# Block 1's attention of a two-block transformer: 64-wide heads handled in pairs on the two array halves

## The chip, the core and the metric

The kernel runs on one core of one Trainium2 chip. The metric is the device time of one execution in microseconds; before the change the median of three runs is 2548.09 us.

## What is computed

Two transformer blocks follow one another on one sequence of 256 tokens of width 2048, in float32. The change touches the first block's attention alone: 16 heads of width 64, whose query chunk of 64 tokens sees up to 9 chunks of 64 keys, with a bias by relative distance. Cut to that part:

```python
h = rms_norm(x, norm_mix_w)
q_a, k_a, v_a, q_g, k_g, v_g, r_g, gate_lr = split_cols(h @ w_in, IN_SPLITS)
# chunked_band_attention, for each chunk c of 64 queries:
s = einsum('bqhd,bkhd->bhqk', qc, kb) * 64 ** -0.5 + bias     # invalid keys: float32's minimum
y_a = einsum('bhqk,bkhd->bqhd', softmax(s), vb)
...
x = x + concatenate([y_a, y_g], axis=-1) @ w_out
# feed forward with a causal convolution, gated embedding; then the second block:
# 8 heads of rotary attention, 8 heads of retention, feed forward, gated embedding
```

With 256 tokens all keys fit: queries 0 to 127 need keys 0 to 127, queries 128 to 255 need keys 0 to 255.

## The kernel before

Every weight is read once from HBM, in 881 tiles of 128 x 1024 numbers at most (`weight_plan`). A tile passes through three stages: SyncE loads it into `raw` (`load`, L148, four buffers), ScalarE copies it to `wh`, rounded to the product format fp32r (`split_hi`, L156, five buffers), and VectorE stores what is left in `wl` (`split_lo`, L167, four buffers). TensorE then multiplies both parts with the activations, which are split in the same way, and sums in PSUM tiles `acc` (`mm`, L222). In `prod_a` (wide tiles of 2 k-tiles and 512 columns) a tile takes 12 products of 512 columns, in `prod_b` 16 of 512 and 256.

The order of all work is that of the Python program. `slot` stands at the start of each weight tile `i`: it emits the rounding of tile `i + 4`, the remainder of tile `i + 3`, the load of tile `i + 7`, and then one `tick`, before the products of tile `i`. A tick takes one step of up to two evictions (`ev`) and one step of the first generator in `side`. Attention is such a generator: its instructions stand in every engine's queue between the work of two weight tiles, and each `yield` passes on to the next tile. Every engine runs its queue in order.

Block 1's mixer (`mix1`) first makes the values, keys and queries of a gated linear attention and runs that as side work (`gla`, whose step `second` holds products with 64-row operands and whose step `third` has products with 64-column weights), then makes `qT` and `kT` (the transposed queries and keys; two heads of 64 share one 128-partition block) and starts `att1`, while the weight products for `va` (the values) and for the gate `rg` run. In one step `s` of `att1` three heads are at work:

- `late` first runs what was put off: the normalisation of the probabilities of head `s - 1` (`softmax`'s `rest`, VectorE, L640 and L642), and the low part of a finished `y1a` block (L667).
- `turn(s - 2)` transposes the probabilities `aP` on TensorE (three transposes, L650) into the one `tr` bank of PSUM, and ScalarE copies them to `aT` (L652).
- `scores(s)` makes the scores of head `s` in a bank `sc` (two banks): 128 and 256 columns on one 64-row half of the array. VectorE adds the bias `aB` and takes the maximum (L628), ScalarE takes the exponential with its sum (L635).
- `values(s - 4)` multiplies with `va`: 256 and 128 columns, with 64-column weights, into one half of the partitions of `pv`; after an odd head ScalarE copies the block to `aV` and rounds it to `y1a` (L663, L664).

`fetch` brings the bias of a pair of heads (L586) and masks a corner on GpSimd (L587). The buffers: `aP`, `aT` and `aB` two, `ast` (the small statistics) three. `softmax` and `turn` are used by block 2's attention too, and block 2 uses the tag `aP` for `qkn` and `sT`.

Of the kernel before, what the change touches and what calls it, by code (L numbers as in the profile page):

```python
# [12 lines left out]
P = 128  # L13
T = 256
# [4 lines left out]
FMIN = float(np.finfo(np.float32).min)  # L19
# [3 lines left out]


def weight_plan():
    """The weight tiles in the order of use: (k-tiles, column ranges).

    Wide tiles have 2 k-tiles of 512 columns (moving operand), narrow ones
    4 k-tiles of 256 columns (stationary operand).
    """  # L30
    tiles = []
    full = tuple(range(KT))

    def gemm(n, kts, chunks):
        for ch in chunks:
            for i in range(0, len(kts), n):
                tiles.append((kts[i : i + n], ch))

    def even(name, lo, hi, step):
        return [[(name, c, c + step)] for c in range(lo, hi, step)]  # L40

    def wide(name, lo, hi):
        gemm(2, full, even(name, lo, hi, 512))

    def narrow(name, lo, hi, kts=full):
        gemm(4, kts, even(name, lo, hi, 256))

    def ffn(gate, up, off, down):
        for a, b in HALVES:
            gemm(4, full, [[(gate, c * P, c * P + P), (up, off + c * P, off + c * P + P)] for c in range(a, b)])  # L50
            narrow(down, 0, D, tuple(range(a, b)))

    def ple(gate, proj):
        for c in range(0, D, 512):
            narrow(gate, c, c + 512)
            gemm(2, (0, 1), even(proj, c, c + 512, 512))

    gemm(2, full, [[("w_in", 4096, 4608)], [("w_in", 4608, 4864)], [("w_in", 4864, 5120), ("w_in", 6144, 6160)]])
    narrow("w_in", 3072, 4096)
    narrow("w_in", 0, 2048)  # L60
    wide("w_in", 2048, 3072)
    wide("w_in", 5120, 6144)
    narrow("w_out", 0, D, MIX_ORDER)
    ffn("w_ffn_up", "w_ffn_up", FF, "w_ffn_down")
    ple("w_ple_gate", "w_ple_proj")
    wide("w_in_2", 0, 3072)
    narrow("w_in_2", 3072, 5120)
    wide("w_in_2", 5120, 7168)
    narrow("w_o_2", 0, D)
    ffn("w_gate_2", "w_up_2", 0, "w_down_2")  # L70
    ple("w_ple_gate_2", "w_ple_proj_2")
    return tiles
# [25 lines left out]
class Net:  # L98
# [14 lines left out]
        self.nacc = 0  # L113
        self.forced = []

# [1 line left out]
    def t(self, tag, shape, dt=F32, bufs=1, name=None):  # L117
        return self.sp.tile(shape, dt, tag=tag, name=name or tag, bufs=bufs)

# [12 lines left out]
    def pv(self):  # L132
        return self.psum("pv", 1)

# [1 line left out]
    def cut(self, i, part):  # L136
        f = self.offs[i][1]
        return slice(0, f) if part is None else slice(part * f // 2, (part + 1) * f // 2)
# [37 lines left out]
        assert len(self.plan[i][0]) == nk  # L176
        return self.H.pop(i), self.L.pop(i), self.offs[i][1] // nk

# [1 line left out]
    def step(self, q, g):  # L180
        try:
            next(g)
# [27 lines left out]
        while key not in self.done:  # L210
            yield

# [1 line left out]
    def begin_chunk(self):  # L214
        c = self.nacc
        self.nacc += 1
# [48 lines left out]
                    self.mm(o, x[:, ls], H[:, sl], False, g + j == nk - 1)  # L265

    def join(self, acc, dst):
        """dst = the sum of both halves of a narrow chunk's accumulators."""
        m = self.v2(self.t("tq", [P, 512], bufs=2))
        self.nc.scalar.activation(m, acc[:, :, T:], AF.Copy)  # L270
        yield
        self.nc.vector.tensor_add(dst, m, acc[:, :, :T])
# [4 lines left out]

        self.ev.append(self.freeing(c, evict(acc)))

# [1 line left out]
    def v2(self, ap):  # L281
        return ap.rearrange("p (b t) -> p b t", b=2)

# [79 lines left out]

        return rc, rb, run()

# [1 line left out]
    def consts(self):  # L367
        nc, ins = self.nc, self.ins
        self.vec = self.t("vec", [P, NV])
# [75 lines left out]
        while self.ev or self.side:  # L445
            self.tick()

# [1 line left out]
    def mix1(self, acts):  # L449
        nc = self.nc  # L450
        rc, rb = self.rc, self.rb
# [125 lines left out]

    def att1(self, qT, kT, va, Y0):
        nc = self.nc
        bias, Pm, PT, st = {}, {}, {}, {}  # L580
        late = []

        def fetch(g):
            if g < 8:
                b = self.t("aB", [P, 2, T], bufs=2)
                nc.sync.dma_start(b, self.ins["bias"][:, 2 * g : 2 * g + 2, :])  # L586
                nc.gpsimd.memset(b[0:64, :, 192:256], FMIN)  # L587
                bias[g] = b

        def scores(h):  # L590
            if h % 2 == 0:
                fetch(h // 2 + 1)
            b = bias[h // 2][:, h % 2, :]
            hp, blk = slice((h % 2) * 64, (h % 2) * 64 + 64), h // 2
            s = self.sc()
            self.mm(s[:, 0:128], qT[hp, blk, 0:128], kT[hp, blk, 0:128], True, True)
            self.mm(s[:, 128:384], qT[hp, blk, 128:256], kT[hp, blk, :], True, True)
            late.append(self.softmax(h, s, [b[:, 128:256], b], FMIN, Pm))

        fetch(0)  # L600
        yield from self.wait(("kT", 3))
        yield
        yield
        for s in range(21):
            if s >= 4:
                yield from self.wait(("va", min(s - 4, 15) // 8))
            while late:
                late.pop(0)()
            if 2 <= s < 18:
                self.turn(s - 2, Pm, PT)  # L610
            if s < 16:
                scores(s)
            if 4 <= s < 20:
                h = s - 4
                if h % 2 == 0:
                    st["pv"] = self.pv()
                self.values(h, PT, va, st["pv"][(h % 2) * 64 : (h % 2) * 64 + 64], slice(h * 64, h * 64 + 64))
                if h % 2 == 1:
                    late.append(self.hilo_plain(Y0, h // 2, st["pv"][:, :T], "y"))
            yield  # L620

    def softmax(self, h, s, masks, floor, Pm, scale=(None, None)):
        nc = self.nc
        p = self.t("aP", [P, 384], bufs=2)
        st = self.t("ast", [P, 8], bufs=3)
        segs = ((0, 128), (128, 384))
        for i, (a, b) in enumerate(segs):
            nc.vector.tensor_tensor_reduce(p[:, a:b], s[:, a:b], masks[i], 1.0, floor, ALU.add, ALU.max, st[:, i : i + 1])  # L628
        if scale[0] is None:
            nc.vector.tensor_scalar(st[:, 2:4], st[:, 0:2], -1.0, None, ALU.mult)  # L630
        else:
            for i in range(2):
                nc.vector.tensor_scalar(st[:, 2 + i : 3 + i], st[:, i : i + 1], scale[i], -1.0, ALU.mult, ALU.mult)
        for i, (a, b) in enumerate(segs):
            nc.scalar.activation(p[:, a:b], p[:, a:b], AF.Exp, bias=st[:, 2 + i : 3 + i],  # L635
                                 scale=1.0 if scale[i] is None else scale[i], accum_out=st[:, 4 + i : 5 + i])
        Pm[h] = p

        def rest():
            nc.vector.reciprocal(st[:, 6:8], st[:, 4:6])  # L640
            for i, (a, b) in enumerate(segs):
                nc.vector.tensor_scalar(p[:, a:b], p[:, a:b], st[:, 6 + i : 7 + i], None, ALU.mult)  # L642
        return rest

    def turn(self, h, Pm, PT):
        nc = self.nc
        p = Pm.pop(h)
        t = self.tr()
        for i in range(3):
            nc.tensor.transpose(t[:, i * P : i * P + P], p[:, i * P : i * P + P], self.ident)  # L650
        o = self.t("aT", [P, 384], bufs=2)
        nc.scalar.activation(o, t[:, :384], AF.Copy)  # L652
        PT[h] = o

# [132 lines left out]
        self.done.add(("go", 3))  # L787
        yield

# [1 line left out]
    def ffn(self, blk):  # L791
        nc = self.nc
        hk = self.hkey
# [79 lines left out]
            yield from self.put_g(G, gk, cl, w[:, 1, :])  # L873
        return ev

# [1 line left out]
    def embed(self, blk):  # L877
        nc = self.nc
        s8 = self.t("S8a", [P, 2, 1024], name="pr")
# [92 lines left out]
            yield  # L972
        self.done.add(("ple", blk, c))

# [1 line left out]
    def rope_tables(self):  # L976
        nc, ins = self.nc, self.ins
        tabs = self.tabs = self.t("g4", [P, 4, 2, P], name="tabs")
        ra = self.t("tq", [P, 512], bufs=2, name="ropeA")
        ra = ra.rearrange("p (s t d) -> p s t d", s=2, t=2)  # L980
        nc.sync.dma_start(ra, ins["ropeA"])
        qk = self.t("aP", [P, 384], bufs=2, name="qkn")[:, :T].rearrange("p (a d) -> p a d", a=2)
        nc.sync.dma_start(qk, ins["qkn"])
        for _ in range(8):
            yield
        for i in range(2):
            nc.vector.tensor_mul(tabs[:, 2 * i], ra[:, 0], self.bc2(qk[:, i, :]))
            for h in range(2):
                a, b = slice(h * 64, h * 64 + 64), slice(64 - h * 64, 128 - h * 64)
                nc.vector.tensor_mul(tabs[:, 2 * i + 1, :, a], ra[:, 1, :, a],  # L990
                                     qk[:, i, b].unsqueeze(1).broadcast_to([P, 2, 64]))
            yield
# [231 lines left out]
    def ret2(self, R4, rv, st):  # L1224
        nc = self.nc
        o = self.t("S8a", [P, 2, 1024], name="ro")
# [15 lines left out]
        def decayed(h):  # L1242
            fetch(h + 1)
            dk = dks.pop(h)
            q, k = R4[:, 0, h], R4[:, 1, h]
            s = self.sc()
            self.mm(s[:, 0:256], k[:, 0:128], q[:, :], True, True)
            self.mm(s[:, 256:384], k[:, 128:256], q[:, 128:256], True, True)
            d = self.t("aP", [P, 384], bufs=2, name="sT")
            nc.vector.tensor_mul(d, s[:, :384], dk)  # L1250
            sT[h] = d

# [119 lines left out]
```

## Time and profile before

| | us |
|---|---|
| three runs | 2547.77, 2548.09, 2548.92 |
| span of the profiled execution (the page gives no other time of it) | 2547.2 |
| TensorE busy | 2534.5 |
| VectorE busy | 1668.3 |
| ScalarE busy | 1282.9 |
| DMA, mean | 184 GB/s |
| block 1's attention as side work | 218.7 to 317 of the span |

The span runs from the first to the last instruction of one profiled execution. Times inside it count from its start. In a timeline a row is one instruction, or several of one kind in a row (x3), with its start and length; matmuls overlap, so the distance from start to start tells what one costs, not its length. Each float32 product appears as two matmuls (two passes), a product in fp32r as one.

### The profile page before, as it was taken

The page shows a single profiled execution, that of the slowest core. Times are in us where ns is not written, and L with a number is a line of the kernel's source. Part 1 is how long each engine was busy: PE and PEld are TensorE (multiplying, and loading weights), DVE is VectorE, ACT ScalarE, POOL GpSimd, SP SyncE. Part 2 cuts the span into 40 slices and gives each one's busy share as a digit, 9 for nine tenths or more (in the row PEclk, how much of TensorE's full clock was granted, in tenths as well). Part 3 has the DMA queues.
Part 4 walks back from the last instruction along what each step waited for, and adds up shares of the span by engine and source line. Part 5 has one row for each costly group of instructions (what it writes and reads, how often), then busy time and mean ns, then how long its engine had stood idle before and what let it go on. Part 6 is the DMA issues. An engine that isn't in the chain of part 4 may idle for free.

```text
span 2547.2 us, 36496 instructions
## 1 busy us (share of the span) xinstructions
PE 2534.5 (100%) x14162; PEld 2184.4 (86%) x14162; DVE 1668.3 (65%) x2374; ACT 1282.9 (50%) x1713; POOL 8.3 (0%) x60
## 2 busy tenths in 40 slices
PE   8999999999999999999999999999999999999999
PEld 7887788888888888888878888888888888888888
DVE  6655567777755777767886775666666555666665
ACT  6534544655543565545544544444444334444443
POOL 0000000000000000000000000000000000000000
PEclk9999999999999999999999999999999999999999
DMA  7545355555555555555555455555555555555554
GB/s 242 183 142 178 131 177 188 187 186 190 190 189 188 186 190 190 192 193 187 189 174 188 161 177 189 174 187 189 188 188 189 190 190 189 187 188 193 190 193 147
DMA packets 133550, 469.30 MB, mean 184 GB/s; under 512 B 14960, under 2 KB 17392, under 8 KB 133376
## 3 DMA queue, kind: packets, MB, share of 16 engines
q1 hardware_dynamic: 133232, 466.95, 54.1%
q8 instruction: 111, 1.82, 0.3%
q14 instruction: 63, 0.52, 0.1%
q10 hardware_dynamic: 144, 0.01, 0.0%
HBM read 464.80 MB, written 2.10 MB: 183 GB/s over the span
## 4 chain that ended last, share of the span: by engine, by line
PE 99%; DMA 0%; DVE 0%; ACT 0%; issue 0%; SPq 0%; ACTq 0%
PE acc L222 95%; PE sc L222 2%; PE pv L222 1%; PE tr L650 0%; DMA raw<-weights 0%; PE sc L1099 0%; ACT wh L156 0%; PE sc L1182 0%; PE sc L528 0%; DVE ty L948 0%; SPq L390 0%; DVE wl L167 0%; DVE X L949 0%; PE tr L737 0%; SPq L148 0%
## 5 line engine op out<-in xcount | busy, mean ns | idle before, releaser
L167 DVE TENSOR_TENSOR wl<-raw,wh 128x1024 fp32r<-128x1024 f32 (+1 forms) x881 | 1068.8, 1214 | 830.6 <-PE acc L222 538.6
L156 ACT ACTIVATE wh<-raw 128x1024 fp32r<-128x1024 f32 (+1 forms) x881 | 924.7, 1050 | 905.7 <-PE acc L222 729.8
L222 PE MATMUL acc<-f,wh 128*128 128x512 f32 x2816 | 984.3, 393 | 0.0
L222 PE MATMUL acc<-f,wl 128*128 128x256 f32 x2816 | 786.2, 279 | 0.0
L222 PEld LDWEIGHTS acc<-f,wh 128*128 128x128 f32 x2816 | 528.0, 187 | 123.9
L222 PEld LDWEIGHTS acc<-f,wl 128*128 128x128 f32 x2816 | 528.3, 188 | 0.0
L222 PE MATMUL acc<-g,wh 128*128 128x512 f32 x1408 | 491.0, 393 | 0.0
L222 PE MATMUL acc<-g,wl 128*128 128x256 f32 x1408 | 393.2, 279 | 0.0
L222 PEld LDWEIGHTS acc<-g,wh 128*128 128x128 f32 x1408 | 264.1, 188 | 61.1
L222 PEld LDWEIGHTS acc<-g,wl 128*128 128x128 f32 x1408 | 264.3, 188 | 0.0
L222 PE MATMUL acc<-hp,wh 128*128 128x512 f32 x512 | 179.9, 394 | 0.0
L222 PE MATMUL acc<-hp,wl 128*128 128x256 f32 x512 | 143.0, 279 | 0.0
L222 PEld LDWEIGHTS acc<-hp,wh 128*128 128x128 f32 x512 | 96.0, 188 | 22.2
L222 PE MATMUL acc<-wh,m2b 128*128 128x512 f32 x320 | 104.5, 398 | 0.0
L222 PE MATMUL acc<-wh,m2a 128*128 128x512 f32 x320 | 104.4, 399 | 0.0
L222 PEld LDWEIGHTS acc<-hp,wl 128*128 128x128 f32 x512 | 96.1, 188 | 0.0
L849 ACT ACTIVATE ty<-tU,vec 128x256 f32<-128x256 f32 x88 | 48.1, 595 | 75.1 <-DVE tU L845 75.1
L270 ACT ACTIVATE tq<-acc 128x512 f32<-128x512 f32 x124 | 71.9, 580 | 4.9 <-PE acc L222 4.9
L222 PE MATMUL acc<-wh,h0a 128*128 128x512 f32 (+2 forms) x224 | 68.1, 380 | 5.7 <-ACT wh L156 5.7
L222 PEld LDWEIGHTS acc<-wh,m2a 128*128 128x128 f32 x320 | 60.3, 188 | 14.2
L222 PEld LDWEIGHTS acc<-wh,m2b 128*128 128x128 f32 x320 | 60.1, 188 | 14.1
L222 PE MATMUL acc<-h0a,wh 128*128 128x512 f32 x192 | 68.6, 397 | 0.0
(272 smaller groups left out, 2780.6 us busy)
## 6 DMA issues: line engine op xcount, KB each, us to landing
raw<-weights SPq DMA_DIRECT2D x863, 512.0 KB, 3.4
raw<-weights SPq DMA_DIRECT2D x10, 256.0 KB, 2.8
raw<-weights SPq DMA_DIRECT2D x8, 272.0 KB, 2.8
aB<-bias SPq DMA_DIRECT2D x8, 256.0 KB, 3.5
X<-xT SPq DMA_DIRECT2D x7, 256.0 KB, 6.6
dk<-decay SPq DMA_DIRECT2D x8, 192.0 KB, 3.7
out<-X SPq DMA_DIRECT2D x6, 256.0 KB, 2.8
pr<-pT SPq DMA_DIRECT2D x2, 256.0 KB, 4.2
```

Of the source, the lines that this page charges most:

```text
L156: self.nc.scalar.activation(self.H[i][:, a], self.raw[i][:, a], AF.Copy)
L167: self.nc.vector.tensor_sub(self.L[i][:, a], r[:, a], self.H[i][:, a].bitcast(F32))
L222: self.nc.tensor.matmul(out, lhsT, rhs, start=start, stop=stop, skip_group_check=True, **kw)
L270: self.nc.scalar.activation(m, acc[:, :, T:], AF.Copy)
L849: nc.scalar.activation(y[:, b, :], u[:, b, 0:T], AF.Identity, scale=self.col("cw0", j), bias=self.col("b_ffn_conv", j))
```

## The change

`att1` now works on pairs. `scores(g)` takes both `sc` banks and issues the 256 columns of head 2g, those of head 2g + 1, and then the 128 columns of each; the two heads lie on the two row halves of the array. `values(g)` does so with the two column halves. A round `g` takes two ticks: the first holds the put-off normalisations, one `turn` and a pair of scores, the second a pair of values and one `turn`. `aP` and `aT` get four buffers, `ast` six. The rest of the diff removes comments and sets a smaller scratch for descriptors of software-made DMAs.

```diff
-        bias, Pm, PT, st = {}, {}, {}, {}
+        bias, Pm, PT = {}, {}, {}
...
-        def scores(h):
-            if h % 2 == 0:
-                fetch(h // 2 + 1)
-            b = bias[h // 2][:, h % 2, :]
-            hp, blk = slice((h % 2) * 64, (h % 2) * 64 + 64), h // 2
-            s = self.sc()
-            self.mm(s[:, 0:128], qT[hp, blk, 0:128], kT[hp, blk, 0:128], True, True)
-            self.mm(s[:, 128:384], qT[hp, blk, 128:256], kT[hp, blk, :], True, True)
-            late.append(self.softmax(h, s, [b[:, 128:256], b], FMIN, Pm))
+        def scores(g):
+            fetch(g + 1)
+            pair, sss = (2 * g, 2 * g + 1), []
+            for h in pair:
+                sss.append((self.sc(), slice((h % 2) * 64, (h % 2) * 64 + 64)))
+            for qs, ks, o in ((slice(128, 256), slice(0, 256), slice(128, 384)), (slice(0, 128), slice(0, 128), slice(0, 128))):
+                for s, hp in sss:
+                    self.mm(s[:, o], qT[hp, g, qs], kT[hp, g, ks], True, True)
+            for h, (s, _) in zip(pair, sss):
+                b = bias[g][:, h % 2, :]
+                late.append(self.softmax(h, s, [b[:, 128:256], b], FMIN, Pm))
+
+        def values(g):
+            o = self.pv()
+            ps = [PT.pop(h) for h in (2 * g, 2 * g + 1)]
+            for t, (lo, ks) in enumerate(((0, slice(0, 256)), (P, slice(256, 384)))):
+                for j in range(2):
+                    h = 2 * g + j
+                    self.mm(o[j * 64 : j * 64 + 64, lo:T], va[:, t, h * 64 : h * 64 + 64], ps[j][:, ks], t == 0, t == 1)
+            late.append(self.hilo_plain(Y0, g, o[:, :T], "y"))
...
-        for s in range(21):
-            if s >= 4:
-                yield from self.wait(("va", min(s - 4, 15) // 8))
+        for g in range(10):
             while late:
                 late.pop(0)()
-            if 2 <= s < 18:
-                self.turn(s - 2, Pm, PT)
-            if s < 16:
-                scores(s)
-            if 4 <= s < 20:
-                h = s - 4
-                if h % 2 == 0:
-                    st["pv"] = self.pv()
-                self.values(h, PT, va, st["pv"][(h % 2) * 64 : (h % 2) * 64 + 64], slice(h * 64, h * 64 + 64))
-                if h % 2 == 1:
-                    late.append(self.hilo_plain(Y0, h // 2, st["pv"][:, :T], "y"))
-            yield
+            if g >= 2:
+                self.turn(2 * g - 3, Pm, PT)
+            if g < 8:
+                scores(g)
+            yield
+            if g >= 2:
+                yield from self.wait(("va", (g - 2) // 4))
+                values(g - 2)
+            if 1 <= g < 9:
+                self.turn(2 * g - 2, Pm, PT)
+            yield
+        while late:
+            late.pop(0)()
...
-        p = self.t("aP", [P, 384], bufs=2)
-        st = self.t("ast", [P, 8], bufs=3)
+        p = self.t("aP", [P, 384], bufs=4)
+        st = self.t("ast", [P, 8], bufs=6)
...
-        o = self.t("aT", [P, 384], bufs=2)
+        o = self.t("aT", [P, 384], bufs=4)
...
-    nc = _bacc.Bacc("TRN2", target_bir_lowering=False, num_devices=1)
+    nc = _bacc.Bacc("TRN2", target_bir_lowering=False, num_devices=1, dynamic_dma_scratch_size=2048)
```

The order of instructions is written by the program, so the rows below show what moves. TensorE's queue before, one tick in the middle of the attention, between the products of two weight tiles (`tr` transposes, `sc` scores, `pv` values, `acc` weight products; a float32 product is one row here):

```order
L222 MATMUL acc<-wh,h0b 128x512
L650 MATMUL tr<-ident,aP 128x128 x3
L222 MATMUL sc<-qk_138 128x128
L222 MATMUL sc<-qk_138 128x256
L222 MATMUL pv<-aT,va 64x256
L222 MATMUL pv<-aT,va 64x128
L222 MATMUL acc<-wh,h0b 128x512
```

The same queue after the change, first a tick with a pair of values:

```order
L222 MATMUL acc<-wh,h0b 128x512
L222 MATMUL pv<-aT,va 64x256 x2
L222 MATMUL pv<-aT,va 64x128 x2
L660 MATMUL tr<-ident,aP 128x128 x3
L222 MATMUL acc<-wh,h0b 128x512
```

and the next, with a pair of scores:

```order
L222 MATMUL acc<-wh,h0b 128x512
L660 MATMUL tr<-ident,aP 128x128 x3
L222 MATMUL sc<-qk_138 128x256 x2
L222 MATMUL sc<-qk_138 128x128 x2
L222 MATMUL acc<-wh,h0b 128x512
```

Two ticks that each held the transposes, scores and values of one head have become one with the values of two heads and one with the scores of two; each keeps one head's transposes.

ScalarE's queue before, one tick of the same part in which a block of `y1a` is finished (`wh` the rounding of a weight tile, `aP` exponentials, `aT` the copy of transposes, `aV` and `y1a` the finished block):

```order
L156 ACTIVATE wh<-raw 128x1024
L652 ACTIVATE aT<-tr 128x384
L635 ACTIVATE aP,ast<-aP,ast 128x128
L635 ACTIVATE aP,ast<-aP,ast 128x256
L663 ACTIVATE aV<-pv 128x256
L664 ACTIVATE y1a<-aV 128x256
L156 ACTIVATE wh<-raw 128x1024
```

and after, from the score tick on through the value tick:

```order
L156 ACTIVATE wh<-raw 128x1024
L662 ACTIVATE aT<-tr 128x384
L645 ACTIVATE aP,ast<-aP,ast 128x128
L645 ACTIVATE aP,ast<-aP,ast 128x256
L645 ACTIVATE aP,ast<-aP,ast 128x128
L645 ACTIVATE aP,ast<-aP,ast 128x256
L156 ACTIVATE wh<-raw 128x1024
L473 ACTIVATE va<-acc,rc 128x512
L673 ACTIVATE aV<-pv 128x256
L674 ACTIVATE y1a<-aV 128x256
L662 ACTIVATE aT<-tr 128x384
```

The exponentials of two heads stand together behind the score tick's copy, and the next `wh` and the value tick's copies stand behind both; the row of `va` is an eviction that falls into this pair of ticks and not into most.

## Rows read from the trace of the kernel before

**Rows 1.** The page, busy time by engine and the chain that ended last, by engine.
```profile
PE 2534.5 (100%) x14162; PEld 2184.4 (86%) x14162; DVE 1668.3 (65%) x2374; ACT 1282.9 (50%) x1713; POOL 8.3 (0%) x60
...
PE 99%; DMA 0%; DVE 0%; ACT 0%; issue 0%; SPq 0%; ACTq 0%
```

**Rows 2.** Timeline of TensorE, one middle tick; columns start us, length us, instruction.
```profile
262.81 0.39 PE L222 MATMUL acc<-wh,h0b 128*128 128x512 f32 x1
263.04 0.49 PE L650 MATMUL tr<-ident,aP 128*128 128x128 f32 x3
263.46 0.92 PE L222 MATMUL sc<-qk 64*128 64x128 f32 x4
264.31 0.86 PE L222 MATMUL pv<-aT,va 128*64 128x256 f32 x4
265.10 0.50 PE L222 MATMUL acc<-wh,h0b 128*128 128x512 f32 x1
265.44 0.40 PE L222 MATMUL acc<-wl,h0b 128*128 128x512 f32 x1
```

**Rows 3.** Timeline of TensorE, an early tick with scores alone.
```profile
222.25 0.39 PE L222 MATMUL acc<-wh,h0a 128*128 128x512 f32 x1
222.58 0.92 PE L222 MATMUL sc<-qk 64*128 64x128 f32 x4
```

**Rows 4.** Timeline of TensorE, products with 64-row operands in the gated linear attention.
```profile
127.73 0.48 PE L222 MATMUL pv<-vg,gke 64*128 64x256 f32 x1
127.73 0.48 PE L222 MATMUL tr<-vg,gke 64*128 64x256 f32 x1
128.05 0.38 PE L222 MATMUL pv<-vg,gke 64*128 64x256 f32 x1
128.06 0.38 PE L222 MATMUL tr<-vg,gke 64*128 64x256 f32 x1
128.26 0.59 PE L222 MATMUL pv<-vg,gke 64*128 64x256 f32 x2
128.79 0.50 PE L222 MATMUL acc<-h0a,wh 128*128 128x512 f32 x1
```

**Rows 5.** Timeline of TensorE, products with 64-column weights in the gated linear attention.
```profile
136.13 1.08 PE L222 MATMUL sc<-gS,gla 128*64 128x256 f32 x6
137.13 0.50 PE L222 MATMUL acc<-h0b,wh 128*128 128x512 f32 x1
```

**Rows 6.** Timeline of VectorE, one slot, and the start of the next.
```profile
263.06 1.23 DVE L167 TENSOR_TENSOR wl<-raw,wh 128x1024 fp32r<-128x1024 f32 x1 [2.33 <-PE acc L222]
264.20 0.16 DVE L640 RECIPROCAL ast<-ast 128x2 f32<-128x2 f32 x1
...
264.86 0.42 DVE L667 TENSOR_TENSOR y1a<-aV,y1a 128x256 fp32r<-128x256 f32 x1
265.20 0.28 DVE L628 CUSTOM_DVE_ANT_0 aP<-sc,aB 128x128 f32<-128x128 f32 x1
...
265.87 0.17 DVE L630 TENSOR_SCALAR ast<-ast 128x2 f32<-128x2 f32 x1
268.04 1.23 DVE L167 TENSOR_TENSOR wl<-raw,wh 128x1024 fp32r<-128x1024 f32 x1 [2.00 <-PE acc L222]
```

**Rows 7.** Timeline of ScalarE, an eviction of va, and later one slot.
```profile
238.68 0.66 ACT L473 ACTIVATE va<-acc,rc 128x512 f32<-128x512 f32 x1
...
258.26 1.06 ACT L156 ACTIVATE wh<-raw 128x1024 fp32r<-128x1024 f32 x1 [1.15 <-PE acc L222]
260.23 0.49 ACT L652 ACTIVATE aT<-tr 128x384 f32<-128x384 f32 x1 [0.91 <-PE pv L222]
260.76 0.40 ACT L635 ACTIVATE aP<-aP,ast 128x128 f32<-128x128 f32 x1
...
261.65 0.36 ACT L663 ACTIVATE aV<-pv 128x256 f32<-128x256 f32 x1
262.05 0.42 ACT L664 ACTIVATE y1a<-aV 128x256 fp32r<-128x256 f32 x1
```

**Rows 8.** DMA issues of the page, the bias; the last number is us to landing.
```profile
aB<-bias SPq DMA_DIRECT2D x8, 256.0 KB, 3.5
```

More of the change, by code (lines that the diff above doesn't have):

```diff
@@ L981, in rope_tables @@
         nc.sync.dma_start(ra, ins["ropeA"])
-        qk = self.t("aP", [P, 384], bufs=2, name="qkn")[:, :T].rearrange("p (a d) -> p a d", a=2)
+        qk = self.t("aP", [P, 384], bufs=4, name="qkn")[:, :T].rearrange("p (a d) -> p a d", a=2)
         nc.sync.dma_start(qk, ins["qkn"])
@@ L1248, in decayed @@
             self.mm(s[:, 256:384], k[:, 128:256], q[:, 128:256], True, True)
-            d = self.t("aP", [P, 384], bufs=2, name="sT")
+            d = self.t("aP", [P, 384], bufs=4, name="sT")
             nc.vector.tensor_mul(d, s[:, :384], dk)
```

## The prediction

> **What bounds the kernel now.** The page comes first: TensorE is busy for 2534.5 of 2547.2 us and holds 99% of the chain that ended last [rows 1]. So a microsecond counts only if it leaves TensorE's own row of work, or adds a wait to it. The change sits in one stretch, block 1's attention (218.7 to 317 us), where the attention runs as side work between the weight products: before each weight tile's 12 products (`acc`, one every 0.23 us, 2.8 us for a tile) TensorE does one tick of attention. I call a tile with its tick a slot. The timeline of TensorE alone shows what a tick costs, read from start to start. Middle slot [rows 2]: from the last product at 262.81 to the transposes 0.23, so no loss; three transposes to the scores 0.42; the scores of one head 0.85; the values of one head 0.79; then the second product comes 0.34 after the first, 0.11 later than usual, because its weights were not loaded ahead. Entering scores straight from a product costs 0.33 instead of 0.23, that is 0.10 [rows 3]. The short attention products thus pay about 0.1 for every change between full-array and half-array work, on the way in and on the way out, beside the columns they stream.
>
> The question that decides is whether two half-array products run at once. The kernel before already has such a place, the gated linear attention [rows 4]. There three products with 64-row operands are issued one whole product after another, each in two passes: `pv` on the lower rows, `tr` on the upper rows, `pv` on the lower rows again. The trace has the first passes of `pv` and `tr` both at 127.73 and the second ones at 128.05 and 128.06, and the third product follows at 128.26. Six passes of 256 columns are over at 128.79, after 1.06 us; in a row they would need about six times 0.215 (the step from 128.05 to 128.26 is 0.21), 1.29, and the changes of mode on top. The same stretch has three products with 64-column weights that write alternate halves of PSUM's partitions: six passes in 1.00 us from 136.13 to 137.13 [rows 5], four passes' worth. So both kinds of pair (rows for scores, columns for values) run in step on this chip.
>
> **The change, part by part.**
> *Scores and values.* `scores(g)` issues 256 columns of head 2g, then of 2g+1, then 128 and 128, in two PSUM banks and the two row halves; `values(g)` does the like in the two column halves. By rows 4 a pair should take the path of one head: 0.85 for scores, 0.79 for values. That halves 16 x 0.85 + 16 x 0.79.
> *Ticks.* Before, with the prices above, the 20 ticks that hold work are: 2 of scores alone (0.10+0.85+0.11 = 1.06), 2 of transposes and scores (0.42+0.85+0.11 = 1.38), 12 of all three (0.42+0.85+0.79+0.11 = 2.17), 2 of transposes and values (0.42+0.79+0.11 = 1.32), 2 of values alone (0.10+0.79+0.11 = 1.00). Sum 2.12+2.76+26.04+2.64+2.00 = 35.56 us. After: 2 ticks of a score pair alone (2.12), 6 of transposes and a score pair (8.28), 3 of transposes alone (0.42 less the 0.10 that a mode change takes, 0.96), 7 of a value pair and transposes, 1 of a value pair alone (1.00). The 7 have the order values, transposes, which no row shows; between 0.10+0.79+0.32 = 1.21 (nothing lost behind) and 1.32 I take 1.32, the price of the same two pieces the other way round, as one entry and one exit remain: 9.24. Sum 21.60. **The ticks give 13.96 us**; some 10.4 of it (16 pairs, each with 2 x 0.215 + 2 x 0.108 = 0.65 of streaming that now runs beside the other head's; 128 columns take half of 256) is overlap, the other 3.6 fewer changes of mode.
> *Transposes.* All 16 stay, each with its copy to `aT`; they move by at most a slot.
> *VectorE.* It does the same work, but both heads' softmax now stands in every second slot, behind that slot's `wl`. From a slot's start [rows 6]: `wl` 1.14, two normalisations of 0.66, the low part of y 0.34, two mask-and-maximum steps of 0.84 (0.67 to the start of the last instruction, which takes 0.17). The first head's scores are ready for the exponential at 3.65, the second's at 4.50. The next slot's `wl` starts about 0.3 late; it is prepared three tiles ahead, so that costs nothing. Per pair of slots VectorE needs 5.6 of 8.3 us (two slots of 2.8, plus 1.38 and 1.32).
> *ScalarE.* A head's exponentials take 0.89 [rows 7], so they end near 5.5; then come `wh` (1.06), `aV` (0.40), `y1a` (0.42) and the copy of the other head's transposes (0.49): the end is near 7.9. What waits for it is TensorE: the single `tr` bank must be empty before the next slot's transposes at 8.3. Cover 0.4 us. In one pair the copy of `va` (0.66) stands in between and overruns this by about 0.3; with a little for the signal I charge **0.4 us**, and between nothing and 2 us for all such waits in the range.
> *Four buffers.* Before, `aT` stood behind the values of the same tick because it had two buffers: 0.9 us of idle ScalarE [rows 7]. With four this wait goes. TensorE did not wait for that copy, so it gives nothing by itself; it is what lets ScalarE fit the shorter slot. In block 2 the softmax, `sT` and `aT` share these tags; TensorE is the chain there too [rows 1], so nothing.
> *Bias.* The 256 KB of a pair's bias are still fetched one pair ahead and land in 3.5 us [rows 8], now with two slots of 4.1 us to do it; on SyncE's queue the fetches stand one or two weight loads from where they stood. Nothing. The smaller scratch for software-made DMA descriptors: no such queue in the profile, nothing.
>
> Sum: 13.96 - 0.4 = 13.6 us. The profiled span of 2547.2 would become 2533.6; the median of the three runs, 2548.09, lies 0.9 above that span, so the forecast is **2534.5 us**. Everything behind shifts forward as it is, since TensorE stays the chain.
>
> **The rivals.**
> *Passes start in program order.* Then only the second pass of one head overlaps the first of the next. A pair then streams first | second and other first | other second and first of the 128 | ... , three steps of 0.215 and two of 0.108 in place of two and two: 0.215 more a pair, 16 x 0.215 = 3.4 us, 2537.9. Against it: rows 4 have `tr`'s first pass 0.32 before `pv`'s second, though `pv`'s was issued first. The Trainium skill states this order (TensorE: Matmul & The Clock Gate, Part 3: Packing small matmuls): matmuls start and end strictly as issued. Here the trace differs from it by those 0.32 us, and the sum goes by the trace. Chance 4%.
> *ScalarE holds the single `tr` bank.* If its chain ends 1 us later than worked out, TensorE waits 0.6 at the transposes; the wait itself lengthens that slot and gives the next pair its cover back, so it comes in every second of 7 pairs: some 2.4 us, 2536.9. For it: only 0.4 us of cover. Against: the terms are measured ones, and ScalarE idles earlier in the pair. 10%.
> *No overlap at all*, so that the pairing is only another order: the path of a score pair becomes 0.85 + 6 x 0.108 = 1.50, of a value pair 1.44; the 16 pairs take back 10.4 us, and 3.2 remain, 2544.9. Rows 4 and 5 speak against. 3%.
> *Slower.* The bias of a pair comes late: VectorE's queue is in order, so the first mask step would hold the next `wl` behind it, and when three tiles of lead are used up TensorE waits. A fetch issued about 1.3 into its slot has until 8.3 + 2.8 = 11.1, near 10 us against 3.5 measured. To undo the gain, each of the 7 later pairs must lose 2 us, so each fetch would have to take some 20 us (10, the lead of about 8, and 2); at 2.7 us lost per pair it is 7 x 2.7 - 13.6 = 5.3 us slower, 2553.4. 2%.
>
> **How the numbers follow.** The forecast holds with 81%, and its own range is 2533.0 to 2536.5 (below: no waits, 0.4, the cheaper order in the 7 ticks, 0.8, and the 0.3 by which the lowest run lies under the median; above: waits of 2 us more). Widened to take in the two milder rivals it is **2533.0 to 2539.0**. What a measurement here can tell from no change is about 0.2%, 5.1 us: the forecast, program order and the `tr` bank all gain more, so faster 0.95; no overlap at all is the same, 0.03; slower 0.02.
>
> **What would show it.** In the changed kernel's timeline, a score pair: passes of both heads starting within 0.02 us of each other, and the next product 0.85 after the first; a value pair 0.79; slots of 4.2 and 4.1 us where 4.98 stood (from `wl` to `wl`, [rows 6]); ScalarE's last copy of a pair ending before the next transposes; TensorE's busy time down by about 13 us. Score passes that start one after another, or a row of waits of TensorE for `aT`, would prove the sum wrong, and a gap before `sc` with VectorE's mask step waiting for the bias the last rival.

## The result, and the profile after

The changed kernel took 2535.19 us in the median of four runs (2530.89, 2532.18, 2538.2, 2539.07), the kernel before beside it 2548.26 (2547.77 to 2548.92, four runs). The ratio is 0.9948, interval 0.9934 to 0.9962: faster by 13.1 us. The four runs of the changed kernel lie on two levels some 7 us apart, though the granted clock is 0.999 or 1.0 in all of them; the experiments come back to this. The profiled execution, 2530.89 us with a span of 2529.1, is one of the lower level.

The page of the changed kernel, busy time by engine, the chain that ended last, and the bias:

```profile
PE 2517.6 (100%) x14162; PEld 2177.6 (86%) x14162; DVE 1667.8 (66%) x2374; ACT 1279.3 (51%) x1713; POOL 8.4 (0%) x60
...
PE 99%; DMA 0%; DVE 0%; ACT 0%; issue 0%; SPq 0%; ACTq 0%
...
aB<-bias SPq DMA_DIRECT2D x8, 256.0 KB, 3.6
```

TensorE stays the chain, and the time left its own work: 2534.5 us busy [rows 1] became 2517.6, 16.9 less, for a span 18.1 shorter. The bias lands as before [rows 8].

The timeline of TensorE, a score tick and the value tick after it, and the start of the next pair:

```profile
251.57 0.39 PE L222 MATMUL acc<-wh,h0b 128*128 128x512 f32 x1
251.80 0.49 PE L660 MATMUL tr<-ident,aP 128*128 128x128 f32 x3
252.22 0.92 PE L222 MATMUL sc<-qk 64*128 64x256 f32 x8
253.07 0.50 PE L222 MATMUL acc<-wh,h0b 128*128 128x512 f32 x1
253.41 0.39 PE L222 MATMUL acc<-wl,h0b 128*128 128x512 f32 x1
...
255.72 0.39 PE L222 MATMUL acc<-wh,h0b 128*128 128x512 f32 x1
256.04 0.87 PE L222 MATMUL pv<-aT,va 128*64 128x256 f32 x8
256.84 0.55 PE L660 MATMUL tr<-ident,aP 128*128 128x128 f32 x3
257.14 0.48 PE L222 MATMUL acc<-wh,h0b 128*128 128x512 f32 x1
257.45 0.39 PE L222 MATMUL acc<-wl,h0b 128*128 128x512 f32 x1
...
259.98 0.49 PE L660 MATMUL tr<-ident,aP 128*128 128x128 f32 x3
```

Eight passes of scores, two heads, take 0.85 us from 252.22 to 253.07: as long as the four passes of one head before [rows 2]. Eight passes of values take 0.80. A pair of slots is 8.18 us long (251.80 to 259.98); two slots before took twice 4.98.

VectorE in the same pair: the remainders `wl`, and between them the last instruction of the second head's mask step.

```profile
251.83 1.23 DVE L167 TENSOR_TENSOR wl<-raw,wh 128x1024 fp32r<-128x1024 f32 x1 [2.62 <-PE acc L222]
...
256.05 0.17 DVE L640 TENSOR_SCALAR ast<-ast 128x2 f32<-128x2 f32 x1
256.15 1.22 DVE L167 TENSOR_TENSOR wl<-raw,wh 128x1024 fp32r<-128x1024 f32 x1
260.01 1.22 DVE L167 TENSOR_TENSOR wl<-raw,wh 128x1024 fp32r<-128x1024 f32 x1 [2.63 <-PE acc L222]
```

Both heads' mask steps fill the first slot to the end, so the second `wl` starts late, at once behind them; the third waits for TensorE again. The slots measured from `wl` to `wl` are 4.32 and 3.86, and nobody waits for the late one.

ScalarE at the end of the same pair:

```profile
257.27 1.04 ACT L156 ACTIVATE wh<-raw 128x1024 fp32r<-128x1024 f32 x1
258.22 0.36 ACT L673 ACTIVATE aV<-pv 128x256 f32<-128x256 f32 x1
258.62 0.42 ACT L674 ACTIVATE y1a<-aV 128x256 fp32r<-128x256 f32 x1
258.94 0.47 ACT L662 ACTIVATE aT<-tr 128x384 f32<-128x384 f32 x1
```

The copy out of the `tr` bank ends at 259.41, 0.57 ahead of the transposes at 259.98. The waits of TensorE's weight loads in the attention (us in total, times, longest) show where that cover did not do:

```profile
PEld tr L660 <- ACT aT L662: 0.7, 2, 0.3
```

**Where the time went, stage by stage.** The attention is only part of it. These rows of TensorE's timeline give the first product of the first feed forward, of block 2's mixer (`m2a`), of its output projection (`y2a`), of the second feed forward and of the second embedding (`hp`). The kernel before:

```profile
426.56 0.40 PE L222 MATMUL acc<-f,wh 128*128 128x512 f32 x1
...
1267.34 0.40 PE L222 MATMUL acc<-wh,m2a 128*128 128x512 f32 x1
...
1612.22 0.39 PE L222 MATMUL acc<-y2a,wh 128*128 128x512 f32 x1
...
1702.83 0.39 PE L222 MATMUL acc<-f,wh 128*128 128x512 f32 x1
...
2440.36 0.40 PE L222 MATMUL acc<-hp,wh 128*128 128x512 f32 x1
```

The changed kernel:

```profile
409.14 0.39 PE L222 MATMUL acc<-f,wh 128*128 128x512 f32 x1
...
1250.19 0.40 PE L222 MATMUL acc<-wh,m2a 128*128 128x512 f32 x1
...
1592.73 0.39 PE L222 MATMUL acc<-y2a,wh 128*128 128x512 f32 x1
...
1682.56 0.39 PE L222 MATMUL acc<-f,wh 128*128 128x512 f32 x1
...
2422.31 0.39 PE L222 MATMUL acc<-hp,wh 128*128 128x512 f32 x1
```

Up to the first feed forward it is 17.4 us ahead, more than the 13.6 forecast; 2.1 of that lie ahead of the first score product (216.57 against 218.72), before any instruction that the change moves. Block 2's mixer, where no instruction moved, then takes 342.54 us (1592.73 - 1250.19) where it took 344.88, and the second feed forward 739.75 where it took 737.53. Stages that the order does not touch changed their pace in both directions, so the prediction's sum cannot be checked against the total alone.

### The profile page after: what moved, and what is told of

Its sections match the earlier page's. It is cut to its first block, busy times and chain, and to the rows that moved or that the text cites. A ratio compares the mean times of both kernels' runs of the same rounds, so it can differ in the third digit from the quotient of the medians.

```text
span 2529.1 us, 36486 instructions
## 1 busy us (share of the span) xinstructions
PE 2517.6 (100%) x14162; PEld 2177.6 (86%) x14162; DVE 1667.8 (66%) x2374; ACT 1279.3 (51%) x1713; POOL 8.4 (0%) x60
## 4 chain that ended last, share of the span: by engine, by line
PE 99%; DMA 0%; DVE 0%; ACT 0%; issue 0%; SPq 0%; ACTq 0%
PE acc L222 95%; PE sc L222 2%; PE pv L222 1%; PE tr L660 0%; DMA raw<-weights 0%; PE sc L1109 0%; ACT wh L156 0%; PE sc L1192 0%; PE sc L528 0%; DVE ty L958 0%; SPq L390 0%; DVE wl L167 0%; DVE X L959 0%; PE tr L747 0%; SPq L148 0%
```

## Experiments

The kernels were measured in three groups (e1 to e4; e5, e6, e7 and e9; e10 to e13), each beside the kernel before and on one chip; medians are given, with the ratio and its interval. The theory was that the order of the pairs gains what the prediction's sum says, by overlap of the two halves; the rivals, that the issue order within a pair, the additional buffers or the place of the buffers in memory made or hid some of it.

### The change again, twice

No edit.

> The changed kernel once more, unaltered. Its four runs lay at 2530.9, 2532.2, 2538.2 and 2539.1 us, while the kernel before keeps within 1.2 us. Theory A (the gain is the ticks of the attention alone, 13.6 us, and the spread is chance): runs spread evenly around 2535. Theory B (beside the ticks, the pace of the weight products changed, and it has two levels): runs fall into two groups near 2531 and 2538.5, with little between.

> The change unaltered, in another call. If the two levels seen so far (2531 in two of the first runs, 2538 in the others) belong to the chip or its day: one level throughout, 2538 or 2531. If they are drawn anew for each loading of the program: both levels among the runs.

Measured: 2538.27 (2537.81 to 2539.72, five runs; before 2547.75; 0.9965, 0.9951 to 0.9978), and on another chip 2538.99 (2537.98 to 2541.0, five runs; before 2548.1; 0.9965, 0.9953 to 0.9978). Both times only the upper of the two levels. Of the second, the three last stage starts:

```profile
1593.87 0.39 PE L222 MATMUL acc<-y2a,wh 128*128 128x512 f32 x1
...
1685.29 0.40 PE L222 MATMUL acc<-f,wh 128*128 128x512 f32 x1
...
2430.53 0.39 PE L222 MATMUL acc<-hp,wh 128*128 128x512 f32 x1
```

Output projection and second feed forward together took 836.66 us here and 829.58 in the changed kernel's first profile; the 7.1 us between the levels lie in these two stages. With ten more runs on the upper level, the first four runs' median of 2535.19 reads as a mixture: two runs near 2531.5 and two near 2538.6.

### The larger buffers without the new order

The scratch alone (e2), and the old order with the change's scratch and buffers (e3):

```diff
-    nc = _bacc.Bacc("TRN2", target_bir_lowering=False, num_devices=1)
+    nc = _bacc.Bacc("TRN2", target_bir_lowering=False, num_devices=1, dynamic_dma_scratch_size=2048)
```

and for e3 also

```diff
-        p = self.t("aP", [P, 384], bufs=2)
-        st = self.t("ast", [P, 8], bufs=3)
+        p = self.t("aP", [P, 384], bufs=4)
+        st = self.t("ast", [P, 8], bufs=6)
...
-        o = self.t("aT", [P, 384], bufs=2)
+        o = self.t("aT", [P, 384], bufs=4)
```

> The kernel before with the smaller descriptor scratch alone. Theory A: 2548.3 within 0.5 us, one level. Theory B (where the tiles lie in SBUF sets the pace of the products, and this edit moves them): another level than 2548, by up to 4 us either way, or two levels.

> The kernel before, attention head by head in the old order, with the smaller scratch and the larger buffer counts (aP 4, aT 4, ast 6), so with the memory map of the changed kernel. Theory A: 2548 within 0.5 us, since TensorE waited for none of these buffers. Theory B: about 4 us less (2544) in the good level, as the products over h0a then take 0.227 us in place of 0.235, and about 2551 in the other.

Measured: e2 2548.16 (eleven runs; 1.0003, 0.9994 to 1.0011), nothing. e3 2552.48 (2551.48 to 2555.09, eleven runs; 1.002, 1.0011 to 1.0028): **the buffers alone cost 4.7 us**. One theory had expected no change, the other 4 us less or 3 more. Against e3, the change measured beside it (e1) is 14.2 us faster. So the new order gains about 14, and something that came with the buffers takes a third of it back.

### Head by head instead of alternately

The pair's products in the order of the heads, as a program that knows nothing of the halves would issue them:

```diff
-            for qs, ks, o in ((slice(128, 256), slice(0, 256), slice(128, 384)), (slice(0, 128), slice(0, 128), slice(0, 128))):
-                for s, hp in sss:
+            for s, hp in sss:
+                for qs, ks, o in ((slice(128, 256), slice(0, 256), slice(128, 384)), (slice(0, 128), slice(0, 128), slice(0, 128))):
...
-            for t, (lo, ks) in enumerate(((0, slice(0, 256)), (P, slice(256, 384)))):
-                for j in range(2):
+            for j in range(2):
+                for t, (lo, ks) in enumerate(((0, slice(0, 256)), (P, slice(256, 384)))):
```

> The changed kernel, but within a pair both products of the first head are issued before both of the second, in scores and in values. If TensorE starts the second head only when its passes come up in the order of issue, a score pair goes from 0.85 to about 1.4 us and a value pair from 0.80 to about 1.35, 16 x 0.55 = 8.8 us more: about 2544. If the two halves have queues of their own that look far enough ahead, the time is that of the changed kernel, 2531 to 2539, with the passes of both heads in step.

Measured: 2538.29 (five runs; 0.9965, 0.9953 to 0.9978), the same as e1 to 0.02 us. TensorE's timeline, the last transpose, then what had started within the first 0.07 us of a score pair:

```profile
251.98 0.27 PE L660 MATMUL tr<-ident,aP 128*128 128x128 f32 x1
252.18 0.49 PE L222 MATMUL sc<-qk 64*128 64x256 f32 x2
```

Two passes stand at 252.18, though three passes of the first head are issued between the first passes of the two; the next weight product follows 0.86 later, at 253.04. The halves fill by themselves: what counts is that the two heads stand next to each other in TensorE's queue, not that they alternate. The rule that the prediction weighed (the Trainium skill, TensorE: Matmul & The Clock Gate, Part 3: Packing small matmuls: matmuls start and end strictly as issued) does not hold for the two halves here: by it the second head's first pass could not have started before the first head's fourth, some 0.64 later (0.32 to the second pass [rows 4], then 0.21 and 0.11). The value pairs, issued head by head as well, start two passes together too, at 255.98, and their ticks are as long as in the change.

### Both heads on one half

The second head's scores are computed from the first head's rows; the odd heads' scores are thus those of the even ones with another bias.

```diff
-                sss.append((self.sc(), slice((h % 2) * 64, (h % 2) * 64 + 64)))
+                sss.append((self.sc(), slice(0, 64)))
```

> The change, but the second head's scores are computed from the first head's rows as well (both heads of a pair use the lower 64 rows, so the odd heads' scores are wrong and so is all that follows from them); same number of products, same order, same memory map. Theory (the pair gains because the two row halves stream at once): the pair's path grows from 0.85 by 2 x 0.215 + 2 x 0.108 = 0.65 to 1.50 us, 8 pairs: +5.2 us against e7_again. Rival (the gain is fewer changes of mode and the order alone): no difference within 0.5 us.

Measured: 2543.3 (eleven runs; 0.9976, 0.9968 to 0.9985), 4.3 us above e7 beside it, where 5.2 were expected. A score tick:

```profile
254.99 1.57 PE L222 MATMUL sc<-qk 64*128 64x256 f32 x8
256.49 0.50 PE L222 MATMUL acc<-wh,h0b 128*128 128x512 f32 x1
```

Within the first 0.11 us of that tick's scores a single pass has started, where e4 shows two:

```profile
254.99 0.48 PE L222 MATMUL sc<-qk 64*128 64x256 f32 x1
```

The pair's path is 1.50 us, the forecast figure without overlap, against 0.85. Changes of mode, order and memory are those of the change, so the 0.65 is the overlap of the halves. From the first score product to the first feed forward e5 takes 197.58 us and e7 192.58: 5.00 us for eight pairs, 0.625 each. That shows the overlap for scores; for values it was not taken away by an experiment, and stands on the pair price of 0.80 and on the two passes with which a pair starts in the changed kernel:

```profile
256.04 0.44 PE L222 MATMUL pv<-aT,va 128*64 128x256 f32 x2
```

### Two aT buffers

```diff
-        o = self.t("aT", [P, 384], bufs=4)
+        o = self.t("aT", [P, 384], bufs=2)
...
-        st = self.t("ast", [P, 8], bufs=6)
+        st = self.t("ast", [P, 8], bufs=3)
```

> The change with two buffers for aT and three for the softmax's small statistics, as before the change (aP keeps four, since in this order four heads are in flight). Theory (the copy of the transposes to aT now stands behind the values in TensorE's own order, so the second pair of buffers is not needed): no new wait of TensorE for aT, block 1's mixer as long as in e7_again within 0.3 us. Rival (the four aT buffers let ScalarE fit the shorter slot): a wait of 0.3 to 0.9 us before the transposes in each of 7 pairs, +2 to +6 us in the mixer. The memory map changes by 3 KB a partition, and with it the pace of the weight products outside the mixer may move: between -7 and +2 us, if the 4.7 us that the larger buffers alone cost in e3_buffers come from addresses.

Measured: 2535.25 (2533.35 to 2535.88, five runs; 0.9948, 0.9935 to 0.9962), 3.7 us faster than the change beside it, with no run as far off as the change's two levels are (it lies some 4 above the change's lower level, which that met in two of its fourteen runs). TensorE's wait for the copy into `aT` is no worse than with four buffers, and ScalarE has no wait for an `aT` buffer:

```profile
PEld tr L660 <- ACT aT L662: 0.5, 2, 0.2
```

So four `aT` buffers are not needed in the new order. (`aP` does need more than two: the probabilities of two heads are still unturned when the next pair's scores come.) The stages of e6:

```profile
411.19 0.40 PE L222 MATMUL acc<-f,wh 128*128 128x512 f32 x1
...
1687.43 0.39 PE L222 MATMUL acc<-f,wh 128*128 128x512 f32 x1
...
2424.96 0.40 PE L222 MATMUL acc<-hp,wh 128*128 128x512 f32 x1
```

The second feed forward takes 737.53 us, to the hundredth what it takes in the kernel before. From the first score product to the first feed forward e6 takes 193.75 us, 1.2 more than e7 and so more than the 0.3 that the expectation allowed; e10 below, with the same two `aT` buffers and the weights where e7 has them, takes 192.56, so this too is the weights' place. The first one starts 15.4 us earlier than before; as the first score product also came 1.3 earlier (217.4 against 218.7), 14.1 of that is the attention.

### The place of the weights

A pool's size is the sum of its buffers, and its tiles lie one behind another. The activations that the weight products read (`h0a`, `f`, `m2a` and the like) lie ahead of `aP`, `ast` and `aT`, so that more of these buffers leave them where they are; the pool of the weights lies behind the whole other pool, so that each buffer of `ast` moves the weights by 32 bytes a partition, one of `aP` or `aT` by 1536, six times 256. Five kernels move the weights and keep the order of all instructions: the weights' pool of the change laid out first (e9), and other numbers of `ast` buffers (e10, e12 and e13 from e6, e11 from the kernel before).

```diff
-    with tc.tile_pool(name="sp", bufs=1) as sp, tc.tile_pool(name="wp", bufs=1) as wp, \
+    with tc.tile_pool(name="wp", bufs=1) as wp, tc.tile_pool(name="sp", bufs=1) as sp, \
```

and, for e10 and e11 (sixteen in e12, eight in e13),

```diff
-        st = self.t("ast", [P, 8], bufs=3)
+        st = self.t("ast", [P, 8], bufs=6)
```

> The change, with the pool of weight buffers laid out in memory ahead of the other pool, so that weights and operands get other addresses; no instruction changes. Theory (the pace of the 512-column products depends on where weights and operands lie): the products of the weight stream change their pace by up to 3%, the total by -7 to +10 us, and block 1's attention ticks keep their prices. Rival (the pace does not hang on addresses): the same time as e7_again within 1 us.

> As e6_aT2, with six instead of three buffers for the softmax's small statistics: every large tile (operands and weights) lies 96 bytes a partition further, that is 96 bytes off in its place within a kilobyte, as in the changed kernel itself, but with 3 KB less of buffers. Theory (the pace of the weight products follows the place within a kilobyte): the pace of the changed kernel comes back, 512-column products on h0a and h0b at 0.227 us where e6_aT2 has 0.235, block 1's mixer 2.4 us shorter than in e6_aT2, the feed-forward stages longer, in total 2538.5 (or 2531, its other level). Rival (the two extra aT buffers or the amount of memory made the difference): 2535.3, as e6_aT2.

> The kernel before, with nothing but six instead of three buffers for the softmax's statistics: 96 bytes a partition. Theory (the place within a kilobyte): 2552.5, as e3_buffers (or some 7 us less, if it meets the other level). Rival: 2548, as before.

> As e6_aT2, with sixteen buffers for the statistics: the large tiles lie 416 bytes further, so that operands and weights begin at a whole kilobyte. Theory: a pace of its own, other than those of e6_aT2 and of the change; no size is known, between 2525 (each stage as fast as the fastest seen in any map: 314 + 90 + 739 + 101 + 341 + 90 + 738 + 101 us and the rest) and 2549. Rival (no such dependence): 2535.3.

> As e6_aT2, with eight buffers for the statistics: 160 bytes further, three quarters of a kilobyte. Theory: as for e12_aT2_ast16, between 2525 and 2549 and different from e6_aT2 by over 1 us; if only the place within 256 bytes counts, equal to e12_aT2_ast16 within 1 us. Rival (no such dependence): 2535.3.

Measured: e9 2548.7 (eleven runs; 1.0003, 0.9994 to 1.0011); e10 2538.08 with one run of five at 2531.13 (0.996, 0.9947 to 0.9974); **e11 2552.96** with one run of eleven at 2545.97 (1.0017, 1.0009 to 1.0026); e12 2549.81 (eleven runs; 1.0006, 0.9998 to 1.0015); e13 2549.15 (eleven runs; 1.0004, 0.9995 to 1.0013). Ninety-six bytes of additional statistics make the old kernel 5.0 us slower, and the layouts of e9, e12 and e13 take back the whole gain of the new order (e12 lies just above the 2525 to 2549 expected). The second feed forward of e11, and two stages of e12:

```profile
1698.06 0.40 PE L222 MATMUL acc<-f,wh 128*128 128x512 f32 x1
...
2443.30 0.39 PE L222 MATMUL acc<-hp,wh 128*128 128x512 f32 x1
```

```profile
411.12 0.40 PE L222 MATMUL acc<-f,wh 128*128 128x512 f32 x1
...
1260.85 0.39 PE L222 MATMUL acc<-wh,m2a 128*128 128x512 f32 x1
```

In e11 the stage takes 745.24 us, to the hundredth that of e7, which shares its 96 bytes and not its attention. In e12 the first feed forward with its embedding takes 849.73 where the kernel before has 840.78.

It is no wait: the products of the feed forwards have no idle time ahead of them. Those of 512 columns themselves take a little longer; in the second feed forward the next product starts 231 ns after such a one in the kernel before and 235 in e11, on average. These products of both feed forwards, in the kernel before and then in e11 (count, busy us, mean ns, idle us before them):

```profile
L222 PE MATMUL acc<-f,wh 128*128 128x512 f32 x2816 | 984.3, 393 | 0.0
L222 PE MATMUL acc<-f,wh 128*128 128x512 f32 x2816 | 990.4, 397 | 0.0
```

Taken from the same view for all kernels, the stages fall into three groups by where the weights begin in a partition, counted from the last multiple of 256 bytes (in the programs as built `raw` begins at byte 174816 before, 174912 in e11, 163552 in e6, 166720 in the change, 163968 in e12, 163712 in e13 and 2176 in e9):

| weights begin, modulo 256 bytes | kernels | feed forward 1 and embedding | mixer 2 | feed forward 2 |
|---|---|---|---|---|
| 224 (as before) | before, e2, e6 | 840.8 | 344.9 | 737.5 |
| 64 (96 further) | change, e1, e3, e4, e5, e7, e10, e11 | 841.0 to 841.3 | 342.5 to 342.6 | 745.2, or 739.8 |
| 128 (160 further) | e9, e12, e13 | 849.7 | 340.7 | 745.7 |

Feed forward 2 has two values in the second group only: 739.8 in the profiles of the change's first runs and of e10, whose executions were on the lower level. The weights of e6 lie 11264 bytes (44 times 256) ahead of those of the kernel before, and e6 has its pace; those of e12 and e13 lie 256 bytes apart and agree, and so does e9, far from both. In e11 the activations stand where they stood, and the products of the feed forwards read nothing else that moved: it is the weights' place that decides. Whether the place of the activations matters as well is open: e9 moves them by 53248 bytes, 208 times 256, and none of these kernels changes their place within 256 bytes. The expectations of e10 and e12 took them to move along, and the weights of e12 to begin at a whole kilobyte; neither is so. Three places of the weights were tried of the eight that steps of 32 bytes allow.

## Why the prediction was right, and where by luck

The forecast was 2534.5 and the median came to 2535.19, inside the range. The mechanism is the forecast one, and its size too. The agreement of the total is better than the working deserves, because the place of the weights moved it by more than the error and in both directions.

- **Pair prices.** 0.85 for scores and 0.80 for values, forecast 0.85 and 0.79. The gated linear attention's products [rows 4, 5] had carried the right answer, and e5 shows what it would have been without overlap.
- **Ticks.** Cleanest between kernels with the weights at the same place, from the first score product to the first feed forward: before 207.84 us, e6 193.75; e11 206.65, e10 192.56; e3 206.64, e1 192.59. The three pairs of kernels give 14.05 to 14.09, against the forecast 13.6.
- **The seven value ticks**, taken at 1.32 with a lower bound of 1.21: the rows above give 1.27 (255.72 to 257.45 is 1.73, less two products of 0.23). That is some 0.3 us of gain more.
- **ScalarE.** Forecast: cover 0.4, one overrun of 0.4 us in all. Measured: cover 0.57, two waits. The two ticks concerned are 0.11 and 0.13 us longer than the other ticks with transposes and scores (1.38), so the price was 0.24. With the value ticks this is about the 0.45 between 13.6 and 14.05.
- **VectorE.** As forecast: the next `wl` starts late and no one waits; 4.32 and 3.86 in place of 4.2 and 4.1, as the late `wl` moves the boundary between the two.
- **Four buffers.** Two claims. That the old order's wait of ScalarE goes, and gives nothing by itself, held (in e3 that wait is gone and nothing is gained). That the four `aT` buffers are what lets ScalarE fit the shorter slot was wrong: with two (e6) nothing waits longer. The reason was argued and not tried: in the new order the transposes stand behind the values on TensorE, so the copy that needs the buffer comes after both anyway.
- **The step that failed** is "TensorE is the chain there too, so nothing" for block 2 and for the buffers, and with it "Everything behind shifts forward as it is". The prediction asked who waits for the buffers and never asked what they push aside. Their 6240 bytes, 96 modulo 256, cost 4.7 us in e3, and 96 alone 5.0 in e11, at the usual level, and gave back about 2 at the lower one (one run of e11, 2545.97). On the level that most runs have, the change is worth 9.5 and 9.1 us (e1, e7), not 13.1. The lowest run, 2530.89, lies under the range's 2533.0, and the upper level, 2538.3 and 2539.0, at its upper end, which had been drawn for other rivals.
- **The rivals.** Program order is refuted by e4, no overlap by the pair prices and e5, the late bias by its 3.6 us. The `tr` bank held by ScalarE is real, in two ticks, at a tenth of its price (0.24 of 2.4 us).
- **The span and busy time.** The forecast 13 us less of TensorE's busy time came out as 16.9: 15.3 from the first score product to the first feed forward (14.1 the order, 1.2 the weights' place, as e11 has it against the kernel before), 1.0 ahead of that stretch and 0.6 behind it, where the later stages' gains and losses of pace nearly cancel at this level.

The version to keep is e6: the pairs with two `aT` and three `ast` buffers, 2535.25 us, 12.85 below the kernel before and 3.7 below the change measured beside it, with less memory. No layout tried holds the lower level of 2531 steadily.

## What to carry to other kernels

When two small products sit on different halves of the array, put them next to each other in TensorE's queue; the order within the pair does not matter, and the gain here is the streaming of one of them plus the saved changes between full-array and half-array work, which another such place in this kernel's trace had already priced. Measure a change that also alters buffer counts twice, once with its buffers and the old order: this kernel, bound by TensorE, lost up to 14.6 us by where its weights came to lie (e12 against e6), as much as the order itself gained, and such a shift shows as a changed pace in stages that the edit does not touch.

## What the hardware showed that was not expected

**The pace of products depends on where the weights lie within 256 bytes.** The 256 rests on e12 and e13; a period of 128 would fit the three places as well, one of 64 not, since places 64 and 128 differ. Between the kernel before and e11 the instructions and their order are the same, and 96 bytes of offset change the second feed forward from 737.53 to 745.24 us, block 2's mixer from 344.88 to 342.59. Why the products take longer no run shows. The Trainium skill (SBUF — State Buffer, SBUF: two separate sides) says that TensorE's port never waits for another engine's; by that the place of the weights should not matter unless TensorE's own reads depend on it, and the traces cannot tell these apart.

**One place has two levels.** With the weights 96 bytes further, an execution takes one of two paces in the last part of the program, 7.1 us apart, with the same instructions: the lower one in two of the first four runs, in none of ten (e1, e7), in one of five (e10), two of eleven (e5), one of eleven (e11), none of eleven (e3) and none of five (e4). It is not the chip: e5 and e7 ran on the same one. In the 11 runs of e2, the 5 of e6, the 33 of e9, e12 and e13 and the 21 to 27 runs of the kernel before in each group nothing like it was seen. What sets the level stays open.

**The two halves run ahead of each other.** Head by head or alternately, both halves start together, within 0.02 us, though in e4 all passes of the one are issued ahead of the first pass of the other. That every engine runs its queue in order, as the description of the kernel before has it, does not hold between TensorE's halves.
